# Other operation times and stated margins in the estimate that places lane steps, in a hybrid encoder layer on one core

## The chip, the cores and the metric

The kernel runs on one core of a Trainium2 chip. The core has a matrix engine (TensorE, PE in the profile), a vector engine (DVE), an activation engine (ACT), a general engine (POOL), a queue that starts most of the DMAs (SP), an on-chip memory (SBUF) and the accumulators of the matrix engine (PSUM, eight banks). Each engine works through its own instructions in the order in which the program lists them and waits on semaphores for the others. The metric is the device time of one execution in microseconds.

## The reference

One layer of a bidirectional encoder is applied to two groups of rows, 1024 sample rows and 256 prompt rows, with shared weights, in float32. All widths are 2048.

```python
hn = rms_norm(x, norm_g)
proj = hn @ w_in                       # 2048 -> 4896, split in nine parts
xbc = silu(centred_dwconv(xbc, conv_w, conv_b))
y = ssd_scan(forward) + ssd_scan(backward) + d_skip * xs     # chunks of 128 rows, 16 heads of 64
o_ssd = rms_norm(y * silu(z_ssd), per group of 512)
o_att = window_attention(q, k, v, sink) * silu(z_att)        # 8 heads, |t-s| <= 128, ALiBi
o_mem = softmax(mq @ mk.T) @ mv * silu(z_mem)                # 4 heads, 256 memory rows
return x + concat([o_ssd, o_att, o_mem]) @ w_out             # 2048 -> 2048
```

Both outputs, for the prompt rows and for the sample rows, are computed.

## The kernel before

The 1280 rows are ten tiles of 128. Tiles 0 to 4 are group 0 and 5 to 9 group 1, and each big projection is done for one group at a time. Every float32 operand of a projection is split into a high and a low part of a one-pass type, and a product is three matmuls (high x high, low x high, high x low). Weights are streamed: SP loads a tile of 128 x 512 into `wraw`, ACT copies it into the high part `wh`, DVE subtracts to get the low part `wl` (`wsplit`, lines 338 to 342).

The program has three parts. In the first, memory keys and values, the first queries, and the gate and convolution columns are projected (`seven_stage` uses seven products instead of eight, with sums of weights made on POOL). The last part is the other group's half of the output projection, in the same way. In between lies the part that the change concerns. There `block_tok` (line 368) projects the rest in blocks of 16 k steps: keys and values, memory queries, `z0` and `z1` for both groups, memory queries again, then the four output blocks of group 0. A block accumulates five row tiles in five PSUM banks (`acc`); each k step issues five times three matmuls. The three other banks, `mix`, are handed round among everything else.

Beside these main matmuls the attention and the scan have to be computed, and their work is cut into steps of Python generators in four lanes (line 252 on): ATT (`attn`, `mem_attn`, `mem_values`), SSD (`ssd_one`, `ssd_two`), PREP (norms, splits and transposes of queries and keys) and DEC (`decay`, the decay matrices of the scan). A step issues a few instructions on PE, ACT, DVE, POOL or SP, then yields what the next step wants: `wants(tiles, banks=..., after=...)` names the tiles that it reads, how many `mix` banks it takes, and earlier steps that must have been issued. A step with `banks` of one begins with matmuls or transposes on PE; one without has only ACT, DVE or POOL work.

When a step is issued decides where its instructions stand in every engine's queue. `pump` (line 301) is called after each group of three main matmuls and issues steps as long as `may` lets one through, in the order ATT, PREP, SSD, DEC. `may` asks whether the lane is owed a step by its rate, whether the `after` names have been issued, and `clk.ready`. If a step must be there and is not, `settle` and `force` issue it without that question: in `refill_o`, before the operand of an output block is loaded, and for all that is left after k step 9 of the third output block (lines 1788 to 1793).

`clk` (`Clocks`, line 43) is an estimate kept while the program is written out; nothing of it runs on the chip. It has a clock for each engine. Every instruction adds `cost` to its engine's clock, which is never behind PE's. Inside lane steps it also keeps, by tile, `full` (when what was written can be read) and `free` (when the place can be written anew); `took` passes a place's `free` on to the next tile in it, and `opens` says when the next `mix` bank is open. SP's loads are put at 2600 ns plus 1.5 ns an element of a partition. `ready` compares with PE's clock: a step goes if its tiles are full, its banks open, and ACT's and DVE's clocks at most `QUEUE`, 4000 ns, ahead. Steps without banks may go `AHEAD`, 300 ns, before their tiles are full. Steps that yield nothing to want (all of the first part's) are never held by `ready`.

The Tile framework then gives the instructions their semaphores; `wsplit` is issued with a higher priority, so that it can stand before lane work that was written out earlier.

Of the kernel before, what the change touches and what calls it, by code (L numbers as in the profile page):

```python
# [30 lines left out]

RATES = {'kv': (4, 4), 'mq0': (8, 8), 'z0': (8, 8), 'z1': (8, 8), 'mq1': (8, 8), 'o': (8, 8)}
DEBT = 6.0
AHEAD, QUEUE = 300.0, 4000.0
NEG = -1e30

UNITS = (0, 4, 1, 5, 2, 6, 7, 3, 8, 9)
# [5 lines left out]
class Clocks:  # L43
# [17 lines left out]
    def cost(self, e, ins, ops, power):  # L61
        n = max([self.size(x) for x in ops] or [1])
        if e == "PE":
            m = self.size(ops[0])
            one_pass = ops[-1].dtype == F32R or ops[1].dtype == F32R
            return m / 2.4 + 14 if one_pass else max(m / 0.6, 213) + 6
        if e == "DVE":
            return 150 + 1.05 * n
        if e == "ACT":
            return (190 + 0.8 * n if n > 16 else 190) + (190 if len(ins.outs) > 1 else 0)  # L70
        if e == "POOL":
            return 60 + 4.2 * n if n > 16 else 250 + 180 * n if power else 300
        return 50

    def ran(self, e, ins, power=False):
        outs, srcs = [[x.bass_ap for x in xs if hasattr(x, "bass_ap")] for xs in (ins.outs, ins.ins)]
        cost = self.cost(e, ins, outs + srcs, power)
        if e != "SP":
            self.now[e] = max(self.now[e], self.now["PE"])
        if not self.lane:  # L80
            self.now[e] += cost
            return
        at = self.now[e] if e != "SP" else self.now["PE"]
        for x in srcs:
            at = max(at, self.full.get(self.name(x), 0.0))
        for x in outs:
            at = max(at, self.free.get(self.name(x), 0.0))
        if e == "SP":
            end = at + 2600 + self.size(outs[0]) * 1.5
        else:  # L90
            end = self.now[e] = at + cost + 20
        for x in srcs:
            k = self.name(x)
            self.free[k] = max(self.free.get(k, 0.0), end)
        for x in outs:
            k = self.name(x)
            if e != "SP":
                self.free[k] = max(self.free.get(k, 0.0), end)
            self.full[k] = end + 90
# [10 lines left out]

    def ready(self, want):
        tiles, n = want[:2]
        at = [self.full.get(self.name(x), 0.0) - (0 if n else AHEAD) for x in tiles]
        at += [self.opens("mix", 3, i + 1) - 400 * i for i in range(n)]
        at += [self.now[e] - QUEUE for e in ("ACT", "DVE")]
        return max(at) <= self.now["PE"]

# [1755 lines left out]
```

## Time and profile before

| What | Value |
|---|---|
| Median of 3 runs | 1775.78 us (1773.38 to 1777.44) |
| Profiled execution | 1773.83 us, span 1772.1 us, granted clock 1.000 |
| PE busy | 1755.3 us, 99% of the span |
| DVE, ACT, POOL busy | 1310.9, 971.8, 683.8 us |
| Main matmuls beside the lanes, PE start to start | 0.23 us each, 512 columns |

A page shows one execution. Rows of groups give the line, the engine, the operation, the tiles written and read, the shapes, a count, busy time and mean duration, then the idle time of the engine just ahead of them and what ended it. All instructions go through one helper, so that their line is always L128, and the tile names tell them apart: `acc` and `accm` are the projections, `psc`, `ppt` and `po` scores, transposes and values of the windowed attention, `pms`, `pmt` and `pmo` the same of the memory attention, `pcb`, `pxs`, `pyf`, `pst`, `py`, `pyb` and `pr` belong to the scan, `pq`, `pk`, `pmq`, `pmk` to the preparation of queries and keys. A float32 matmul in several passes shows as two records. The end of a matmul is modelled: it is pipelined, and the next one starts well before it.

### The profile page before, as it was taken

How to read it: one execution, taken by the hardware profiler on the slowest of the kernel's cores; microseconds unless marked ns; L12 is line 12 of the kernel's file. 1: busy time of each engine (PE TensorE's matmuls, PEld its weight loads, DVE VectorE, ACT ScalarE, POOL GpSimd, SP SyncE). 2: the span in 40 equal slices, each digit the busy share in tenths (PEclk: the TensorE clock that was granted, in tenths of full speed). 3: DMA queues.
4: the chain of work that ended last, by engine and by line, in shares of the span. 5: the costliest groups of instructions: out<-in, count | busy, mean ns of one | idle time of the engine just before them, and what ended most of it. 6: DMA issues, size and time to landing. Idle time of an engine off the chain costs nothing.

```text
span 1772.1 us, 30974 instructions
## 1 busy us (share of the span) xinstructions
PE 1755.3 (99%) x10306; PEld 1572.0 (89%) x10306; DVE 1310.9 (74%) x2417; ACT 971.8 (55%) x2181; POOL 683.8 (39%) x1092
## 2 busy tenths in 40 slices
PE   9999999999999999999999999999999999999999
PEld 7889999999899999988788877887788888889999
DVE  5596788989968888797777877678776533766665
ACT  6554555445545444346787666658886532433332
POOL 0026798860478989220110000111200100068775
PEclk9999999999999999999999999999999999999999
DMA  8794454446544333376467766767785734644442
GB/s 293 238 319 175 136 149 148 128 143 194 156 119 145 119 104 106 90 216 208 143 188 249 259 213 192 226 190 230 243 249 161 222 110 147 207 142 147 145 144 77
DMA packets 210993, 313.23 MB, mean 177 GB/s; under 512 B 21584, under 2 KB 84368, under 8 KB 210832
## 3 DMA queue, kind: packets, MB, share of 16 engines
q1 hardware_dynamic: 210688, 311.19, 56.7%
q8 instruction: 81, 1.33, 0.3%
q14 instruction: 80, 0.66, 0.1%
q10 hardware_dynamic: 144, 0.06, 0.0%
HBM read 242.42 MB, written 68.75 MB: 176 GB/s over the span
## 4 chain that ended last, share of the span: by engine, by line
PE 88%; DMA 4%; DVE 3%; ACT 2%; issue 1%; POOL 1%; SPq 0%; ACTq 0%; DVEq 0%; POOLq 0%
PE acc L128 66%; PE accm L128 11%; PE py L128 2%; PE po L128 1%; PE psc L128 1%; PE pst L128 1%; PE pmo L128 1%; PE pms L128 1%; PE ppt L128 1%; DMA wraw<-in_w_in_laid_dram 1%; PE pyf L128 1%; DMA xst<-in_x_prompt_dram 1%; DVE wl L128 1%; PE pyb L128 0%; ACT lg L128 0%
## 5 line engine op out<-in xcount | busy, mean ns | idle before, releaser
L128 PE MATMUL acc<-wh,xH 128*128 128x512 f32 (+1 forms) x1248 | 490.0, 393 | 0.1
L128 DVE TENSOR_TENSOR wl<-wraw,wh 128x512 fp32r<-128x512 f32 (+1 forms) x480 | 355.5, 744 | 172.9 <-ACT wh L128 170.1
L128 PE MATMUL acc<-wl,xH 128*128 128x512 f32 (+1 forms) x1248 | 473.7, 380 | 0.7 <-DVE wl L128 0.5
L128 PE MATMUL acc<-wh,xL 128*128 128x512 f32 (+1 forms) x1248 | 472.1, 378 | 0.0
L128 ACT ACTIVATE wh<-wraw 128x512 fp32r<-128x512 f32 (+1 forms) x480 | 291.5, 613 | 211.6 <-PE acc L128 136.5
L128 POOL TENSOR_TENSOR ws<-wraw 128x128 f32<-128x128 f32 x224 | 156.9, 700 | 365.8 <-DMA wraw<-in_w_in_pairs_dram 163.1
L128 PEld LDWEIGHTS acc<-wl,xH 128*128 128x128 f32 x1248 | 234.7, 188 | 45.1 <-issue 6.5
L128 PEld LDWEIGHTS acc<-wh,xH 128*128 128x128 f32 x1248 | 234.6, 188 | 44.9 <-issue 7.0
L128 PEld LDWEIGHTS acc<-wh,xL 128*128 128x128 f32 x1248 | 234.2, 188 | 44.6 <-issue 1.0
L128 ACT ACTIVATE sh<-ws 128x384 fp32r<-128x384 f32 x224 | 115.5, 522 | 253.3 <-POOL ws L128 126.6
L128 DVE TENSOR_TENSOR sl<-ws,sh 128x384 fp32r<-128x384 f32 x224 | 158.7, 712 | 115.4 <-ACT sh L128 113.9
L128 POOL TENSOR_TENSOR ws<-wraw,ws 128x128 f32<-128x128 f32 x224 | 153.1, 683 | 17.2
L128 POOL TENSOR_TENSOR ws<-ws,wraw 128x128 f32<-128x128 f32 x224 | 154.3, 689 | 0.0
L128 POOL TENSOR_TENSOR wraw<-wraw 128x128 f32<-128x128 f32 x224 | 139.8, 624 | 17.1
L128 PE MATMUL acc<-xH,wl 128*128 128x320 f32 x320 | 100.0, 312 | 1.0 <-DVE wl L128 1.0
L128 PE MATMUL acc<-tH,sl 128*128 128x320 f32 x320 | 98.9, 309 | 0.0
L128 PE MATMUL acc<-xL,wh 128*128 128x320 f32 x320 | 98.9, 309 | 0.0
L128 PE MATMUL accm<-tH,wl 128*128 128x320 f32 x320 | 98.8, 309 | 0.0
L128 PE MATMUL acc<-tH,sh 128*128 128x320 f32 x320 | 98.7, 309 | 0.0
L128 PE MATMUL acc<-xH,wh 128*128 128x320 f32 x320 | 98.7, 309 | 0.0
L128 PE MATMUL accm<-tL,wh 128*128 128x320 f32 x320 | 98.5, 308 | 0.0
L128 PE MATMUL accm<-tH,wh 128*128 128x320 f32 x320 | 98.5, 308 | 0.0
(458 smaller groups left out, 3829.1 us busy)
## 6 DMA issues: line engine op xcount, KB each, us to landing
wraw<-in_w_in_pairs_dram SPq DMA_DIRECT2D x160, 256.0 KB, 2.7
wraw<-in_w_in_laid_dram SPq DMA_DIRECT2D x128, 256.0 KB, 3.6
wraw<-in_w_out_laid_dram SPq DMA_DIRECT2D x64, 256.0 KB, 3.1
wraw<-in_w_out_pairs_dram SPq DMA_DIRECT2D x64, 256.0 KB, 2.9
rf<-ac SPq DMA_DIRECT2D x40, 256.0 KB, 3.8
rb<-ac SPq DMA_DIRECT2D x40, 256.0 KB, 4.2
wraw<-in_w_mem_laid_dram SPq DMA_DIRECT2D x32, 256.0 KB, 4.7
ra<-in_x_turned_dram SPq DMA_DIRECT2D x16, 320.0 KB, 3.8
```

Source lines behind the costliest of these rows:

```text
L128: r = f(*a, **kw)
```

## The change

It touches constants and three functions of `Clocks`, nothing else. The costs of PE, DVE and ACT instructions are stated anew: a one-pass matmul is at least 85 ns, a float32 one counts by the share of its 128 output rows; DVE is 67 + 1.04 ns a column; ACT is 50 from PSUM or 92 from SBUF, plus 0.835 a column, 92 for each operand that is a tile beyond the first, and 92 for an accumulated sum. In a lane step the engine's clock now moves by the cost alone, and what it wrote or read is ready or free 110 ns (ACT) or 90 ns (DVE) later, where it was 20 for both clock and tile. In `ready` a step with banks waits until 700 ns after its tiles are full, a step without banks until they are full (not 300 ns before), and a bank counts as open 300 ns after its estimate.

```diff
-AHEAD, QUEUE = 300.0, 4000.0
+MARGIN, QUEUE = {"PE": 700.0, "bank": 300.0, "other": 0.0}, 4000.0
+LATE = {"ACT": 110.0, "DVE": 90.0}
...
             one_pass = ops[-1].dtype == F32R or ops[1].dtype == F32R
-            return m / 2.4 + 14 if one_pass else max(m / 0.6, 213) + 6
+            return max(m / 2.4 + 14, 85) if one_pass else max(m / 0.6, 213) * list(ops[0].ap)[0][1] / 128 + 6
         if e == "DVE":
-            return 150 + 1.05 * n
+            return 67 + 1.04 * n
         if e == "ACT":
-            return (190 + 0.8 * n if n > 16 else 190) + (190 if len(ins.outs) > 1 else 0)
+            aps = sum(hasattr(x, "bass_ap") for x in ins.ins)
+            return (50 if ops[-aps].space == "PSUM" else 92) + 0.835 * n + 92 * (aps - 1) + (92 if len(ins.outs) > 1 else 0)
...
         if e == "SP":
             end = at + 2600 + self.size(outs[0]) * 1.5
         else:
-            end = self.now[e] = at + cost + 20
+            self.now[e] = at + cost
+            end = at + cost + LATE.get(e, 20)
...
         tiles, n = want[:2]
-        at = [self.full.get(self.name(x), 0.0) - (0 if n else AHEAD) for x in tiles]
-        at += [self.opens("mix", 3, i + 1) - 400 * i for i in range(n)]
+        at = [self.full.get(self.name(x), 0.0) + MARGIN["PE" if n else "other"] for x in tiles]
+        at += [self.opens("mix", 3, i + 1) - 400 * i + MARGIN["bank"] for i in range(n)]
         at += [self.now[e] - QUEUE for e in ("ACT", "DVE")]
         return max(at) <= self.now["PE"]
```

## The prediction

> **What bounds the kernel now.** I began with the first and fourth part of the page: busy time, then the chain of work that ended last.
>
> ```profile
> span 1772.1 us, 30974 instructions
> PE 1755.3 (99%) x10306; PEld 1572.0 (89%) x10306; DVE 1310.9 (74%) x2417; ACT 971.8 (55%) x2181; POOL 683.8 (39%) x1092
> ...
> PE 88%; DMA 4%; DVE 3%; ACT 2%; issue 1%; POOL 1%; SPq 0%; ACTq 0%; DVEq 0%; POOLq 0%
> ```
>
> TensorE (PE) is busy for all but 1772.1 - 1755.3 = 16.8 us. The change issues the same instructions as before in another order, so PE's own work stays, and what it can win are PE's waits. The planner's `ready` is asked only for steps that state wants, and these lie between the last projection of keys and values and the output blocks. I took that stretch, and the 46 us behind it, from the table of stages, and then the waits of PE within the first.
>
> ```profile
> 730.00:1446.00 716.00, 706.21 (x3923) 581.08 (x3922) 526.57 (x1187) 479.59 (x1272) 80.46 (x154) 1.00 0.66 204
> 1446.00:1492.00 46.00, 46.00 (x205) 38.06 (x204) 12.40 (x19) 8.25 (x14) 0.00 (x0) 1.00 0.46 140
> ```
>
> ```profile
> engine line waited for: us in total, times, longest us
> PE py L128 <- ACT mpT L128: 2.3, 1, 2.3
> PE ppt L128 <- DVE nm L128: 1.4, 1, 1.4
> PE po L128 <- ACT pT L128: 0.9, 1, 0.9
> PE pms L128 <- DVE mql L128: 0.9, 1, 0.9
> PE pxs L128 <- DMA xc<-xbc_d: 0.8, 1, 0.8
> PE pms L128 <- DVE moT L128: 0.6, 1, 0.6
> PE acc L128 <- DVE wl L128: 0.5, 1, 0.5
> PE pacs L128 <- issue: 0.5, 1, 0.5
> PE psc L128 <- ACT st L128: 0.5, 1, 0.5
> PE pxs L128 <- DVE nm L128: 0.4, 1, 0.4
> PE pr L128 <- DVE y L128: 0.3, 1, 0.3
> PE psc L128 <- ACT pT L128: 0.2, 1, 0.2
> PE psc L128 <- ACT kL L128: 0.2, 1, 0.2
> ```
>
> In the stage (columns: PE, weight loads, DVE, ACT, POOL) PE is idle for 716.00 - 706.21 = 9.8 us; the thirteen rows hold 9.5 of them. That is little more than half a per cent of the span, and it is the whole stake. A wait costs a little more than its idle time, because the matmul ahead of it counts as busy to its end. The neighbourhood of the second row shows it.
>
> ```profile
> 865.93 0.46 PE L128 MATMUL acc<-wh,xH 128*128 128x512 f32 x1
> 866.23 0.39 PE L128 MATMUL acc<-wl,xH 128*128 128x512 f32 x1
> 866.46 0.39 PE L128 MATMUL acc<-wh,xL 128*128 128x512 f32 x1
> 868.23 0.44 PE L128 MATMUL ppt<-identr,lg 128*128 128x128 f32 x2 [1.39 <-DVE nm L128]
> 868.43 0.47 PE L128 MATMUL acc<-wh,xH 128*128 128x512 f32 x1
> 868.74 0.39 PE L128 MATMUL acc<-wl,xH 128*128 128x512 f32 x1
> ```
>
> Undisturbed, the next matmul starts 0.23 us after the one before (866.23 to 866.46) although each lasts 0.39. So every wait costs 0.16 us beside its idle time: thirteen times 0.16 is 2.1, and all waits together are worth 9.5 + 2.1 = **11.6 us**. No placement of the steps can gain much more.
>
> **The terms of the sum.** The new durations first, since both the old and the new rule decide by them. Rows of DVE and ACT working without a pause:
>
> ```profile
> 1083.03 0.68 DVE L128 TENSOR_TENSOR state<-state,cd_all 128x512 f32<-128x512 f32 x1
> 1083.62 0.69 DVE L128 TENSOR_TENSOR ya<-ya,sk 128x512 f32<-128x512 f32 x1
> 1084.22 0.42 DVE L128 CAST kT<-pk 128x256 fp32r<-128x256 f32 x1
> ...
> 1091.91 1.28 ACT L128 ACTIVATE rf<-rf,wj_all 128x128 f32<-128x128 f32 x4 [4.16 <-DMA rf<-ac]
> 1093.10 0.61 ACT L128 ACTIVATE wh<-wraw 128x512 fp32r<-128x512 f32 x1
> ```
>
> From start to start a DVE operation of 512 columns takes 0.59 to 0.60 us. The old estimate is 150 + 1.05 x 512 = 688 ns, plus 20 in a lane; the new is 67 + 1.04 x 512 = 599. Four ACT operations of 128 columns with a bias operand take 1093.10 - 1091.91 = 1.19 us, 0.30 each; old 190 + 102 + 20 = 312, new 92 + 107 + 92 = 291. So the new figures are right for spacing, and the old ones are long by about 100 ns an operation where the operation is wide. With the old ones a queue of k wide operations got about k x 0.1 us of unstated margin; now it gets a fixed one.
>
> [...]
>
> *PE steps that waited for an operand* (`po`, `pms` for `mql`, `pxs` for its load, `pr`): 2.9 us idle + 4 x 0.16 = 3.5. The old rule let them go at the estimated end plus 90 + 20; the new one adds 700 and the lag of the engine.
> - `mql`, one DVE operation of 512: 688 + 110 = 798 before, 599 + 90 + 90 + 700 = 1479 after, 0.68 later. Left of 0.9 + 0.16: 0.4.
> - `po`, two ACT copies of 256 from PSUM: 2 x 415 + 90 = 920 before, 2 x 264 + 110 + 90 + 700 = 1428 after, 0.51 later. Left of 1.06: 0.55.
> - `pxs`: the load's estimate is unchanged, so 0.70 later. Left of 0.96: 0.26. `pr`, like `mql`: nothing left.
>
> Together 3.5 - 1.2 = **2.3 us gained**.
>
> *PE steps that waited for a PSUM place* (the released engine had just emptied one of the three `mix` banks): `py`, `ppt`, `pms` for `moT`, `pxs` for `nm`, three `psc`. For one ACT copy of 512 the place opens at 190 + 410 + 20 = 620 before and 478 + 110 + 300 = 888 after, 0.27 later; with two or three wide operations queued ahead the 100 ns each have eaten that. The five small ones cost 0.6 + 0.5 + 0.4 + 0.2 + 0.2 + 5 x 0.16 = 2.7; at 0.27 less each **1.3 us are gained** if no queue stands ahead, nothing if three do (bounds 0 and 1.3). The two large ones have another cause. `py` waited for `mpT`, which stood on ACT behind the row above that was idle for 4.16 us on a load of the decay rows; the chain shows that load:
>
> ```profile
> 1083.28 8.61 DMA rf<-ac
> ```
>
> The planner gives it 2600 + 768 = 3.4 us, in both versions. What helps is only that a step of ACT or DVE is no longer sent 300 ns ahead of its operand, so that it blocks its engine 0.3 us less: **0.6 us** for the two (`ppt` I count alike, since its releaser on DVE is a long wait too; bounds 0 and 2 x 0.3).
>
> *What is not touched*: `acc` for `wl` and `pacs`, 1.0 us. *PE's estimate*: a transpose of one pass goes from 67 to 85 ns, a value product of 64 output rows from 433 to 219. It slows or speeds the planner's clock by under a microsecond a step, and moves no work.
>
> *Splitting a burst.* Behind a burst of lane steps the second main matmul starts 0.31 us after the first (868.43 to 868.74) instead of 0.23. If margins make two bursts of what was one, 0.08 us is lost; one more for each of the 20 attention and memory steps is 1.6 us, one fewer gains the same. I take 0.
>
> **Later lanes.** Every wait in a chain of steps grows. For attention with 384 keys, by the diff's formulas: scores to exponent 936 to 1112 ns, exponent to sum 1414 to 1488, sum to scaling 134 to 318, scaling to transpose 1124 to 1910, copies to values 1124 to 1642. Four quarters and two halves give 4 x 1.22 + 2 x 0.52 = 5.9 us a step, and 18 places at 0.26 another 4.7. Memory attention: low part to scores 0.68 later, scaling to transpose 0.78, copy to values 0.67, maximum to exponent 0.18, twice each, at most 4.6. This much is lost only if each wait is the last to end; the order written in the kernel interleaves four quarters, and shorter queues give some back, so I take a third: 3.5 and 1.5. Whether that costs time depends on what is behind.
>
> ```profile
> L128 PE MATMUL psc<-kT,qT x80: 274/337/447, 850.9 to 1350.1; 128*128 128x384 f32 x48, 128*128 128x256 f32 x32
> ...
> L128 PE MATMUL pms<-mkH,mqh x40: 276/283/386, 1079.1 to 1434.1; 128*128 128x256 f32 x40
> ...
> 1445.65 126.25 PE acc L128 x561
> ```
>
> First and last starts show one chain of attention steps from 850.9 to about 1445. From then on PE runs 561 main matmuls in 126.25 us, 0.225 each, with nothing between them. The kernel empties the lanes by force after ten k steps of the third output block, which leaves 6 x 15 + 240 = 330 main matmuls, 75 us before 1572, that is at about 1497. The slack is 50 us. The rear half (six attentions, ten memory steps) is late by 6 x 3.5 + 10 x 1.5 = 36 us, 110 by the upper bound. By the value I take it fits, and moving lane work into the plain stretch costs nothing, since that work is PE's own either way.
>
> **The sum.** 2.3 + 1.3 + 0.6 = 4.2 us gained. The profiled execution took 1773.83 us (span 1772.1 and 1.7 around it), so 1769.6 for its like. The median of the runs shown, 1775.78, is 1.95 above it, so I forecast **1771.6 us**, 0.24% faster. From no change a measurement of this kernel can tell about 0.2%, 3.55 us; the forecast lies just past it.
>
> **The rivals.**
> - *All waits go* (14%). The margins are long enough for every row but the load, and fewer bursts gain another 1 us: 1775.8 - 11.6 = 1764. For it: eleven of the thirteen waits are under 1 us. Against: the two largest are not of the estimate's making.
> - *Waits move, and the sum stays* (23%). The waits are thirteen single events; with the steps moved, others meet a late load or a full queue. Long queues have lost their k x 0.1 us: 1775.8 with 2 us to each side.
> - *Lanes too late, slower* (13%). If more than 50 us of delay come together, the steps left at 1497 are forced in order with no main matmul between them. A forced memory step stands on PE for its own chain: two halves of exponents, scaling and a copy, by the ACT rows below 2 x (1.12 + 1.01 + 0.59) = 5.4 us beside DVE's part, about 6. At 60 us too late (110 - 50) some three steps are left, 18 us; I price it at a step and a half with the gain kept half, +9 - 2 = 1783. The same force stands earlier, where the second-scan steps must have been done for the next operand.
>
> ```profile
> L128 ACT ACTIVATE mpr<-pms,mm,mr 128x256 f32<-128x256 f32 x40 | 22.1, 561 | 13.8 <-DVE mm L128 12.4 <-PE pyf L128 0.7 <-DVE mden L128 0.7
> ...
> L128 ACT ACTIVATE mpr<-mpr,mden 128x256 f32<-128x256 f32 x40 | 17.9, 506 | 0.0
> ...
> L128 ACT ACTIVATE mpT<-pmt 128x512 f32<-128x512 f32 x20 | 11.8, 591 | 10.0 <-PE pmt L128 10.0
> ```
>
> - *Deeper queues, slower* (7%). The limit of 4 us on ACT and DVE now holds a sixth more work, so a weight split can stand behind more of it, and the main matmuls wait for `wl`. It decides if that 0.5 us grows beyond the 4.2 gained: ten such waits of 0.9 give 9 - 4.2 = +5, 1781.
>
> **How the numbers follow.** The forecast has 43%, its own range 1768 to 1775; ten of the 43 fall within 0.2%. Faster: 33 + 14 = 47. Same: 10 + 21 of the second rival = 31. Slower: 13 + 7 + 2 = 22. The range runs from all waits gone, 1764, to the forced lanes, 1784.
>
> **What would show it.** PE's idle time in the stage falls from 9.8 to about 6; the rows for `mql`, `pT`, `y` and `xc` shrink or go; a row like `py` for a bank behind a late load remains. The last `pmo` starts later than before, near 1480, and before 1497. ACT's and DVE's operations have the same counts and durations. I am wrong if the waits for banks grow in number, if `wl` leads the list, if lane matmuls stand without main ones between them near 1497, or if the chain of the lanes ends no later than before, which would say that the margins don't set its pace.

## The result: 0.24% slower, and the profile after

The median after is 1781.69 us, against 1776.57 us for the kernel before on the same chips. The ratio is 1.0024 with a 95% interval of 1.0014 to 1.0035. The prediction said 1771.6 us and faster. Two executions in the whole record, at 2551 and 9506 us, are far off all others and count in no ratio and in no median of the table below. The profiled execution after took 1782.1 us. The first rows of its page, span and busy time:

```profile
span 1780.4 us, 30984 instructions
PE 1756.6 (99%) x10306; PEld 1570.4 (88%) x10306; DVE 1309.1 (74%) x2417; ACT 972.0 (55%) x2181; POOL 679.6 (38%) x1092
```

The engines' counts are the same, and PE is idle for 1780.4 - 1756.6 = 23.8 us, where it was 16.8: 7.0 of the 8.3 us between the two spans. (The medians differ by 5.1 us; the profiled execution of the kernel before, 1773.83 us, was one of its quicker ones.) The table of stages (span of the stretch, then PE, weight loads, DVE, ACT, POOL busy) says where. Two rows of the kernel after, and the first stretch of the kernel before, whose second the prediction shows:

```profile
0.00:728.00 728.00, 724.07 (x4465) 686.42 (x4466) 582.26 (x913) 371.30 (x698) 448.59 (x682) 1.00 0.52 165
730.00:1446.00 716.00, 700.71 (x3872) 574.64 (x3871) 523.95 (x1178) 473.90 (x1257) 79.30 (x154) 1.00 0.66 203
```

```profile
0.00:728.00 728.00, 725.65 (x4481) 689.34 (x4482) 584.95 (x916) 371.48 (x698) 451.46 (x682) 1.00 0.53 165
```

Ahead of 728 us the idle time went from 2.4 to 3.9 us. No step is held there, and the two traces list the same PE instructions in the same order up to 761 us, so this 1.6 us is one execution against another; over all profiled runs of this case, which share that order, the idle time there lies between 2.2 and 3.9 us. In the stage with the lanes it went from 9.8 to 15.3, 5.5 us more. That is the loss: from the 4700th to the 8950th matmul of PE, a stretch that holds all the lanes, the kernel after takes 6.1 us longer, which is these 5.5 us and five waits more at the prediction's 0.16. PE's waits there, of the kernel after:

```profile
engine line waited for: us in total, times, longest us
PE pxs L131 <- DMA xc<-xbc_d: 2.5, 2, 2.1
PE pk L131 <- DVE xs L131: 1.6, 1, 1.6
PE pst L131 <- DVE nm L131: 1.6, 1, 1.6
PE pmk L131 <- DMA wraw<-in_w_in_laid_dram: 1.4, 1, 1.4
PE acc L131 <- DVE wl L131: 1.4, 1, 1.4
PE psc L131 <- DVE oT L131: 1.4, 3, 1.0
PE pq L131 <- ACT pT L131: 1.3, 1, 1.3
PE pq L131 <- DVE qh L131: 1.1, 1, 1.1
PE psc L131 <- DVE xs L131: 1.0, 1, 1.0
PE psc L131 <- ACT qT L131: 0.5, 1, 0.5
PE po L131 <- ACT cb L131: 0.4, 1, 0.4
PE pxs L131 <- ACT pT L131: 0.4, 1, 0.4
PE po L131 <- DVE nm L131: 0.3, 1, 0.3
PE ppt L131 <- ACT qT L131: 0.3, 1, 0.3
PE psc L131 <- DVE ya L131: 0.2, 1, 0.2
```

Of the thirteen rows of before only `pxs` for `xc` and `acc` for `wl` are left. `mql`, `y` and the `pT` under `po` are gone, and so are `py` and `ppt` for `nm`. In their place stand others, and there are more of a microsecond.

Two rows are not what their names say. The one of `pmk` names a load of weights, which `pmk` does not read. It reads `mkr`, and DVE's last operation on that ends at 764.98 + 0.69 = 765.67, just ahead of it:

```profile
764.98 0.69 DVE L131 TENSOR_TENSOR mkr<-mkr,gm 128x512 f32<-128x512 f32 x1
...
765.87 0.63 PE L131 MATMUL pmk<-identr,mkr 128*128 128x128 f32 x4 [1.39 <-DMA wraw<-in_w_in_laid_dram]
```

And `pr` for `y` in the kernel before, which the prediction counted as an operand, is a bank: `pr` reads `yd`, while `y` is what DVE makes out of the bank of `pyb`, up to 1220.38, ahead of `pr` at 1220.43. Sorted so by what was awaited (bank: the releaser had just emptied a `mix` bank; `psc` for `qT`, 0.5 us, is counted there, though the copy that empties its bank also makes its operand):

| us of PE idle in the stage | before | after |
|---|---|---|
| a PSUM bank | 5.9 | 9.0 |
| an operand made by ACT or DVE | 1.8 | 2.5 |
| the load of the scan's columns | 0.8 | 2.5 |
| weights, other | 1.0 | 1.4 |
| sum | 9.5 | 15.4 |

What one such wait for a bank is made of shows in the timeline of the second row, DVE first, then PE:

```profile
1021.45 0.75 DVE L131 COPY_PREDICATED rb<-upper,rf 128x512 f32<-128x512 uint32 x1 [2.78 <-DMA rb<-ac]
1022.08 0.68 DVE L131 TENSOR_REDUCE qss<-sq 128x8 f32<-128x512 f32 x1
1022.66 0.68 DVE L131 SCALAR_TENSOR_TENSOR zs<-zs,acc 128x512 f32<-128x512 f32 x1
1023.26 0.42 DVE L131 CAST bth<-pcb 128x256 fp32r<-128x256 f32 x1
1023.59 0.68 DVE L131 COPY xs<-pxs 128x512 f32<-128x512 f32 x1
...
1022.31 0.39 PE L131 MATMUL acc<-wh,xL 128*128 128x512 f32 x1
1024.33 0.37 PE L131 MATMUL pk<-identr,kh 128*128 128x128 f32 x2 [1.63 <-DVE xs L131]
```

DVE stands for 2.78 us before an operation whose load of decay rows is late. Behind it wait four others in order, the last of them the copy that empties the bank; PE comes to `pk` meanwhile and waits for that bank. The estimate of DVE's durations has no part in this: they are right, and DVE was not working. `qh`, the operand under `pq` at 1043.84, is late in a like way: ACT, which makes its high part, had stood for 5.90 us until 1040.90 for a load of decay rows.

### The profile page after: what moved, and what is told of

Its sections match the earlier page's. It is cut to its first block, busy times and chain, and to the rows that moved or that the text cites. A ratio compares the mean times of both kernels' runs of the same rounds, so it can differ in the third digit from the quotient of the medians.

```text
span 1780.4 us, 30984 instructions
## 1 busy us (share of the span) xinstructions
PE 1756.6 (99%) x10306; PEld 1570.4 (88%) x10306; DVE 1309.1 (74%) x2417; ACT 972.0 (55%) x2181; POOL 679.6 (38%) x1092
## 4 chain that ended last, share of the span: by engine, by line
PE 86%; DMA 7%; DVE 2%; ACT 2%; issue 1%; POOL 1%; SPq 0%; DVEq 0%; ACTq 0%; POOLq 0%
PE acc L131 65%; PE accm L131 10%; PE py L131 2%; PE psc L131 1%; PE pst L131 1%; DMA rb<-ac 1%; PE pmo L131 1%; DMA rf<-ac 1%; PE po L131 1%; PE pms L131 1%; DMA sst<-in_x_sample_dram 1%; PE ppt L131 1%; PE pyb L131 1%; PE pyf L131 1%; DMA wraw<-in_w_in_laid_dram 1%
## 5 line engine op out<-in xcount | busy, mean ns | idle before, releaser
L131 POOL TENSOR_TENSOR ws<-wraw 128x128 f32<-128x128 f32 x224 | 152.3, 680 | 375.2 <-DMA wraw<-in_w_in_pairs_dram 167.4
L131 POOL TENSOR_TENSOR wraw<-wraw 128x128 f32<-128x128 f32 x224 | 141.6, 632 | 17.1
L131 POOL TENSOR_TENSOR es<-sinkb,nm 128x2 f32<-128x2 f32 x40 | 12.8, 321 | 234.5 <-DVE nm L131 189.0
```

What stands on the lines that cost most here:

```text
L131: r = f(*a, **kw)
```

## The experiments

Three theories stood at the start. Q: the short durations took the margin that long queues had. L: the margins make the lanes late, and that costs. R: any small change of the planner's constants deals steps, and so waits, anew (a deal is the order in which the steps come to stand), and the kernel before is one of the better deals among its neighbours. The table gives all runs. The ratio is to the kernel before on the same chip, whose medians there were 1775.7 to 1777.1 us; "waits" is the sum of the rows of PE's waits between 728 and 1520 us, "half clock" the time between 728 and 1520 us in which the granted clock was 0.50, "lanes" the start of the last value product of the memory attention. These three are of one profiled execution each. As the executions of one kernel lie up to 8 us apart, they show kinds and rough sizes, and "slower" is said of the ratios.

| Kernel | median us | ratio to before (95%) | waits us | half clock us | lanes us |
|---|---|---|---|---|---|
| before | 1776.6 | 1 | 9.5 | 0 | 1445.4 |
| after | 1781.7 | 1.0024 (1.0014 to 1.0035) | 15.4 | 0 | 1469.4 |
| estimate alone | 1789.9 | 1.0072 (1.0059 to 1.0084) | 14.0 | 6.8 | 1430.7 |
| margins alone | 1790.1 | 1.0075 (1.0063 to 1.0088) | 19.1 | 3.4 | 1496.9 |
| before, ahead 320 | 1781.6 | 1.0030 (1.0019 to 1.0041) | 14.3 | 0 | 1453.5 |
| before, ahead 310 | 1781.6 | 1.0035 (1.0021 to 1.0048) | 13.3 | 0 | 1446.2 |
| before, ahead 290 | 1787.2 | 1.0060 (1.0046 to 1.0074) | 18.9 | 6.8 | 1460.6 |
| before, queue 4100 | 1794.3 | 1.0092 (1.0079 to 1.0105) | 19.2 | 3.4 | 1443.5 |
| after, operands 720 | 1778.6 | 1.0012 (1.0003 to 1.0021) | 10.8 | 0 | 1464.9 |
| after, operands 680 | 1783.1 | 1.0040 (1.0028 to 1.0053) | 16.8 | 0 | 1458.5 |
| after, bank 320 | 1782.4 | 1.0035 (1.0023 to 1.0047) | 15.1 | 0 | 1470.8 |
| after, other -20 | 1783.6 | 1.0041 (1.0028 to 1.0055) | 13.8 | 0 | 1460.9 |
| after, queue 4100 | 1789.8 | 1.0069 (1.0055 to 1.0082) | 21.8 | 3.4 | 1473.8 |
| after, bank 900 | 1778.7 | 1.0010 (1.0002 to 1.0019) | 11.7 | 3.4 | 1464.7 |
| after, loads 5000 | 1793.2 | 1.0099 (1.0086 to 1.0112) | 17.5 | 17.1 | 1518.7 |
| after, other 380 | 1777.6 | 1.0006 (0.9997 to 1.0016) | 8.0 | 0 | 1497.9 |
| after, other 400 | 1774.2 | 0.9984 (0.9975 to 0.9993) | 7.7 | 0 | 1493.5 |
| after, other 420 | 1774.4 | 0.9990 (0.9981 to 0.9999) | 8.8 | 0 | 1494.8 |
| after, other 400, operands 720 | 1784.0 | 1.0040 (1.0028 to 1.0052) | 11.7 | 6.8 | 1494.3 |
| after, other 700 | 1787.3 | 1.0064 (1.0052 to 1.0076) | 16.9 | 3.4 | 1508.3 |

Waits and half clock together account for the stretch of the lanes. From the 4700th to the 8950th matmul of PE, every run differs from the kernel before by its idle time, 0.16 us for each wait and half of its time at half clock, to within 2 us, but for the estimate alone (3.7 us more) and the operands at 720 (2.6 us less).

**The two halves of the change.** The estimate alone, with the old margins:

```diff
-MARGIN, QUEUE = {"PE": 700.0, "bank": 300.0, "other": 0.0}, 4000.0
+MARGIN, QUEUE = {"PE": 0.0, "bank": 0.0, "other": -300.0}, 4000.0
```

> The changed kernel with the old margins (a step without a bank goes 300 ns early, 0 for operands and banks of PE steps): only the new durations and the 110/90 ns of lag are left of the change. Theory Q (the shorter durations took away the margin that long queues had, so PE meets banks and operands that are not ready): slower than the changed kernel, 1785 to 1795 us, with more PE idle time between 730 and 1500 us than its 11 us. Theory L (the margins make the lanes late, and that costs): about the kernel before, 1773 to 1778. Theory R (any new order deals the waits anew): anywhere within 1771 to 1783.

And the margins alone, in the kernel before:

```diff
-AHEAD, QUEUE = 300.0, 4000.0
+MARGIN, QUEUE = {"PE": 700.0, "bank": 300.0, "other": 0.0}, 4000.0
...
-        at = [self.full.get(self.name(x), 0.0) - (0 if n else AHEAD) for x in tiles]
-        at += [self.opens("mix", 3, i + 1) - 400 * i for i in range(n)]
+        at = [self.full.get(self.name(x), 0.0) + MARGIN["PE" if n else "other"] for x in tiles]
+        at += [self.opens("mix", 3, i + 1) - 400 * i + MARGIN["bank"] for i in range(n)]
```

> The kernel before with the new margins alone (700 ns for operands of PE steps, 300 for banks, no going ahead), its long durations kept. Theory Q: faster than before, 1768 to 1773 us, since both margins now stand together and PE's waits nearly go. Theory L: slower, 1780 to 1786, the lanes ending later than in the changed kernel (there 1468 us). Theory R: anywhere within 1771 to 1783.

Both are slower than before by three quarters of a per cent, more than the two together. The first is what Q expected, the second is the opposite of it: with the long durations and the margins, waits rose to 19.1 us. L expected the first near the kernel before. It has the earliest lanes of all, and loses 13 us. No theory of added effects gives these two and their sum. R allowed for either sign, but not for this size: it had 1771 to 1783 us for both.

**One constant moved by next to nothing.** The kernel before with `AHEAD` at 320, 290 and 310 in place of 300, and with `QUEUE` at 4100 in place of 4000:

```diff
-AHEAD, QUEUE = 300.0, 4000.0
+AHEAD, QUEUE = 320.0, 4000.0
```

> The kernel before with one constant moved by next to nothing: steps without a bank may go 320 ns ahead, not 300. Theories Q and L: 1774 to 1778 us, the same within what can be told, PE idle near 10 us in the stage. Theory R: the time moves by 3 us or more to either side, and the list of PE's waits holds other pairs.

> The kernel before, steps without a bank 290 ns ahead, not 300: a second neighbour on the other side. Theory R (a new order deals the waits anew, and the kernel before is a lucky deal): 1778 to 1785 us, as the neighbour at 320 was 1781.6. Theory S (the change itself does the harm, and 320 was an accident): 1775 to 1778.

> The kernel before with steps without a bank 310 ns ahead. Lucky deal: slower, 1779 to 1790. A smooth dependence on the constant with its best place at 300: less than half of what 320 cost, 1776 to 1779.

> The kernel before with ACT's and DVE's clocks allowed 4100 ns ahead of PE's, not 4000. If its 1776 us is a lucky deal among neighbours (320: +5, 290: +11.5), this third neighbour too is slower, 1779 to 1790. If those two were accidents of going ahead, 1774 to 1778.

All four are slower, by 0.30, 0.60, 0.35 and 0.92% (5, 11, 6 and 16 us), on both sides of 300. Ten or twenty nanoseconds of a constant are no mechanism: what they do is to let one step go a pump sooner or later, after which the rest of the lanes stands in another order. With 310, PE's instructions stand in the order of before up to 846 us, and behind that 1713 of its 10306 places hold another. Theory R expected this, and Q and L didn't; the size was beyond it in two runs, 290 (it had up to 1785 us) and the queue (up to 1790). PE's waits of the last of them, the longest rows:

```profile
PE pmt L128 <- ACT mpT L128: 2.3, 1, 2.3
PE psc L128 <- ACT qT L128: 2.3, 3, 1.2
PE pmq L128 <- DVE moT L128: 2.0, 2, 1.3
PE pr L128 <- DVE yd L128: 1.8, 1, 1.8
PE ppt L128 <- DVE nm L128: 1.7, 1, 1.7
```

None of these five stands in the list of before with more than 1.4 us, and four not at all.

The same of the changed kernel: 720 and 680 for the operands of PE steps, 320 for a bank, -20 for the steps without one, and the queue's limit at 4100.

```diff
-MARGIN, QUEUE = {"PE": 700.0, "bank": 300.0, "other": 0.0}, 4000.0
+MARGIN, QUEUE = {"PE": 720.0, "bank": 300.0, "other": 0.0}, 4000.0
```

> The changed kernel with 720 ns of margin for the operands of PE steps, not 700. Theory R: another deal, anywhere within 1774 to 1787 us, 3 us or more from the changed kernel's 1781.7 with even chance, with other pairs in the list of waits. Theory S: 1780 to 1783, the same pairs.

> The changed kernel with 680 ns for the operands of PE steps, the neighbour on the other side of 720 (which gave 1778.6). Theory R: another deal, 1774 to 1788 us, PE's idle time in its page going with it. Theory S2 (the changed estimate gives a steadier result than the old one, near 1781 with 3 us to each side): 1777 to 1784.

> The changed kernel with 320 ns of margin for a PSUM bank, not 300. The order of PE differs from the changed kernel's only from late in the lanes on, less than half as many places as in the other neighbours. Theory R: up to 4 us to either side of 1781.7. Theory S: 1780 to 1783.

> The changed kernel, steps of ACT and DVE alone let go 20 ns ahead of their tiles, not at 0: the same shift that cost the kernel before 5 us. If the two estimates are equally good on the mean of their deals: 1779 to 1793 us, like the neighbours of the kernel before (1781.6 to 1794.3). If the changed estimate is the better one and only compared with a lucky deal: 1777 to 1784, like its three neighbours so far (1778.6 to 1783.1).

> The changed kernel with the limit on ACT's and DVE's clocks at 4100 ns, not 4000: the shift that cost the kernel before 17 us. Equally good: 1779 to 1793 us. Changed estimate better: 1777 to 1784.

They lie at 1.0012, 1.0040, 1.0035, 1.0041 and 1.0069, with the changed kernel's 1.0024 among them: mean 1.0037 of six. The four neighbours of the kernel before have a mean of 1.0054, and 1.0043 with the kernel before itself. So the changed kernel is an ordinary deal of its kind, and the kernel before is better than each of its four neighbours. Whether the new estimate is the better one on the mean stays open: the means differ by 0.0017, or by 0.0006 with both kernels counted in, and the neighbours of either kernel spread by more than that (by 0.0062 for the kernel before, by 0.0057 for the changed one). The last run had been meant to tell it and fell outside what the better estimate was to give.

**More margin for a bank.**

```diff
-MARGIN, QUEUE = {"PE": 700.0, "bank": 300.0, "other": 0.0}, 4000.0
+MARGIN, QUEUE = {"PE": 700.0, "bank": 900.0, "other": 0.0}, 4000.0
```

> The changed kernel with 900 ns of margin for a PSUM bank, not 300. Theory Q: most of the new waits are for banks, so 1773 to 1777 us, and the rows of psc, pk and pq that wait for an engine that empties a bank go. Theory L: slower still, 1784 to 1792, lanes ending beyond 1480 us. Theory R: anywhere within 1773 to 1785.

1.0010 against the changed kernel's 1.0024, some 2.5 us faster, with waits of 11.7 us. Q had said 1773 to 1777 us. The rows of `pk` and `pq` went, that of `psc` did not, others for banks came (`pyb`, `pxs`), and the gain is no more than that of 20 ns of another margin. It tells Q and R apart no better than a coin.

**Loads put at 5000 ns.** Late loads stand at the head of several long waits, so the estimate of a load was raised.

```diff
-            end = at + 2600 + self.size(outs[0]) * 1.5
+            end = at + 5000 + self.size(outs[0]) * 1.5
```

> The changed kernel with a load estimated at 5000 ns plus 1.5 an element, not 2600. PE's waits for the columns of the scan (xc) were 2.5 us in the changed kernel, 4.1 with the margins alone and 2.6 in the neighbour at 320; ACT's and DVE's waits for the decay rows block both in order. Theory D (the unmodelled load is the largest steady cause of PE's waits): 1774 to 1778 us, no wait of PE for xc, and fewer waits of ACT for rf. Theory R: the waits for xc go, others come, within 1775 to 1786.

PE's waits for the scan's columns are no longer in the list, and ACT's for the decay rows went down, first the kernel after, then this one. DVE's for the decay rows did so less, from 12.3 to 9.7 us.

```profile
ACT rf L131 <- DMA rf<-ac: 15.3, 8, 5.9
```

```profile
ACT rf L131 <- DMA rf<-ac: 4.2, 3, 2.1
```

Still it is the slowest of all by its ratio, 1.0099. Here lateness seems to cost, at a place that the prediction named: the second-scan steps must have been issued by k step 11 of the last memory-query block, and those not yet done are forced there. The main matmuls of that k step end at 1236 us in this run, and the second scan (`pyb` and `pr`) follows from there to 1268, with 4.7 us of PE's waits in it. Behind it, up to 1296, stand attention steps with few main matmuls between them and another 6.5 us of waits; that they crowd there because of the force was not shown.

```profile
1200.00:1240.00 40.00, 38.32 (x194) 30.77 (x192) 25.98 (x56) 24.44 (x58) 8.68 (x14) 1.00 0.61 184
1240.00:1300.00 60.00, 50.26 (x217) 34.61 (x217) 46.99 (x97) 34.35 (x82) 10.40 (x22) 0.89 0.81 252
```

The timeline of PE in the second of these stretches:

```profile
1264.00 1.10 PE L131 MATMUL pyb<-state,cc 128*128 128x512 f32 x2 [0.83 <-DVE yd L131]
1275.36 1.62 PE L131 MATMUL pq<-identr,qh 128*128 128x128 f32 x8 [1.18 <-DVE qh L131]
1278.31 2.83 PE L131 MATMUL po<-pT,v_all 128*64 128x256 f32 x12 [1.33 <-ACT qT L131]
1295.03 0.44 PE L131 MATMUL psc<-kT,qT 128*128 128x384 f32 x1 [2.76 <-DVE oT L131]
```

In those 60 us PE is idle for 9.7, nearly as long as in the whole stage of the kernel before (9.8), and its granted clock is 0.89, by an estimate worth 60 x 0.11 = 6.6 us more.

**ACT and DVE steps held longer.** If a step that sits at the head of ACT or DVE with a late operand is the trouble, it can be sent later.

```diff
-MARGIN, QUEUE = {"PE": 700.0, "bank": 300.0, "other": 0.0}, 4000.0
+MARGIN, QUEUE = {"PE": 700.0, "bank": 300.0, "other": 400.0}, 4000.0
```

> The changed kernel with steps of ACT and DVE alone held until 400 ns after their tiles are full, not until they are. Theory H (PE's long waits for banks are steps that sit on ACT or DVE behind one whose operand is late, so holding that one back frees them): 1772 to 1778 us, ACT idle for rf and rb and PE's waits for a bank above 1 us both fewer. Theory L: the lanes end some 30 us later than in the changed kernel's 1470, near the forced end, 1783 to 1795. Theory R: 1775 to 1788 with lanes ending before 1495.

> The changed kernel, ACT and DVE steps held 380 ns after their tiles. If holding them is what helps: 1772 to 1778 us, PE's waits near 8 us like those at 400. If 400 was a lucky deal: 1776 to 1786, waits of 10 to 16 us.

> The same at 420 ns. Holding helps: 1772 to 1778 us. Lucky deal: 1776 to 1786, or more if the last steps are forced in the third output block (at 400 the last lane matmul stood at 1491.7 us).

> Held 400 ns, and 720 ns for operands of PE steps. Holding helps: 1771 to 1778 us. Lucky deal: 1776 to 1786.

> Held 700 ns. The lanes ended 24 us later at 400 than at 0, so here some 18 us later again, past k step 9 of the third output block: one or two memory steps are forced, with no main matmuls in a gap of about 4 us each (as in the run with loads at 5000 ns). Lateness past the forced end costs: 1778 to 1786 us, and fewer waits ahead of it than in the changed kernel. It does not: 1770 to 1776.

At 400 the kernel is faster than both, 0.9984 of before. PE's waits of that run, the longest:

```profile
PE pr L131 <- ACT pT L131: 1.7, 1, 1.7
PE acc L131 <- DVE wl L131: 1.3, 2, 0.7
PE pyb L131 <- DVE moT L131: 1.1, 1, 1.1
```

The neighbours at 380 and 420 have as few waits, 8.0 and 8.8 us, and 1.0006 and 0.9990, better than any neighbour at 0. So far holding helps. But with 720 for the operands beside it the time is 1.0040, and at 700 it is 1.0064, so it is no steady gain either. The reason given for it fell: ACT's wait for the decay rows was 16.7 us at 400, not less than the 15.3 of the changed kernel. In the run at 700 the lanes did end past the forced place, at 1508, and lost nothing there; its waits lie ahead. The expectation for it spoke of gaps of 4 us without main matmuls, and there are none. In five runs lane matmuls stand behind the place of the last force: 24 in those held 380, 400, 420 and 700 with operands at 700, and 60 in the run with loads at 5000. Main matmuls stand between them, and PE is busy for all of the 74 us from 1446 to 1520 in each, so the last force cost no idle time in any run.

## Why the prediction was wrong, point by point

**The step that failed** is the sum over the thirteen rows. It took each wait of before, lengthened the planner's rule for it by 0.27 to 0.70 us, and counted what was left. That holds a wait as one event which stays in its place while its length changes. It doesn't stay: the first step that goes one pump later changes every queue behind it, and the runs of the kernel before with 10 and 20 ns show that this alone moves the sum of the waits from 9.5 to between 13 and 19 us. In the changed kernel it is 15.4. The prediction had this as its second rival, with "the sum stays", 2 us to each side and 23%. That size was wrong: the four neighbours of the kernel before are 5 to 16 us slower, all to one side, as the kernel before had fewer waits than they. The profile of one kernel could not show that; but a list of single events, two of which hold 40%, could have warned of it.

- *Durations.* Right for the rows that were compared: in the kernel before the DVE rows of 512 columns at 1083 us, of 0.68 and 0.69 us, start 0.59 and 0.60 ahead of the next, where the new figure is 0.599, and in the kernel after the two at 1022.08 and 1022.66 do so 0.58 and 0.60 ahead. That made no kernel faster: the estimate alone is slower by 0.72%.
- *Operands of PE steps.* The rows that were to shrink are gone: `mql`, `pT` under `po`, and `y`, which was a bank. But two others came, `qh` under `pq` and `mkr` under the first `pmk`, and the kind went from 1.8 to 2.5 us. The load `xc` was to shrink to 0.26 and is 2.5.
- *Banks.* The rows counted as banks held 5.6 us and were to lose 1.9, of which 1.3 was the upper of its two bounds; measured 9.0. This is the term that grew most, and its sign was wrong.
- *What is not touched.* `wl` and `pacs` were to stay at 1.0 us. `wl` alone is 1.4, and `pacs` is not in the list.
- *Later lanes.* The last `pmo` record was to move by 36 us to about 1480, and moved by 24 to 1469. That the slack would hold is confirmed, and that lateness in itself costs nothing fits the runs: the earliest lanes of all (1430.7, estimate alone) belong to a kernel 13 us slower, and the fastest has them at 1493.5. The rows, before, after, estimate alone, and held 400:

```profile
L128 PE MATMUL pmo<-mpT,mv x160: 271/275/328, 1099.7 to 1445.4; 128*128 128x128 f32 x160
```

```profile
L131 PE MATMUL pmo<-mpT,mv x160: 271/275/342, 1102.4 to 1469.4; 128*128 128x128 f32 x160
```

```profile
L131 PE MATMUL pmo<-mpT,mv x160: 271/275/343, 1088.3 to 1430.7; 128*128 128x128 f32 x160
```

```profile
L131 PE MATMUL pmo<-mpT,mv x160: 271/275/377, 1126.9 to 1493.5; 128*128 128x128 f32 x160
```

- *The rivals.* "Waits move, and the sum stays" had the cause and not the sum. "Lanes too late" is not what happened: they ended at 1469, ahead of the forced place, which the main matmuls put at 1503 in this run. Its price of about 6 us for a forced memory step was seen in no run either. "Deeper queues" has a little for it, as `wl` waits 1.4 us and not 0.5, but one wait of that size is not the ten that it counted. Of the signs that were to show the forecast wrong, one came: the waits for banks grew in number, from 8 to 13.
- *The bound of 11.6 us* on any gain held: the best kernel is 2.9 us below the kernel before in its own runs (1774.2 against 1777.1).
- *The price of a wait*, idle time plus 0.16, is too low for some long ones: behind one of 2.3 us stood 3.4 us at a clock of 0.51, as the last section shows.

## What to carry to other kernels

Where an order is made by a greedy rule over estimated times, compare a change with the neighbours of the kernel before, not with the one kernel: move a constant by a hair a few times, and see how far the time goes. If that spread is larger than the effect looked for, a list of waits is a sample of single events, and the working out of each row's change is not a forecast. Where the kernel before turns out better than all its neighbours, as here, any new deal, also one from a truer estimate, is likely to start with a loss: of the nineteen other kernels here, sixteen are slower beyond their interval. Why the kernel before is so good a deal is not known.

## What the runs showed of the hardware that was not expected

**Half clock behind some waits.** In the kernel before with the queue's limit at 4100, four stretches of 3.4 us around the wait of `pmt` (PE's busy time first, the granted clock third from the end):

```profile
1086.70:1090.10 3.40, 3.40 (x26) 3.04 (x24) 2.31 (x6) 2.16 (x7) 1.43 (x2) 1.00 0.94 332
1090.10:1093.50 3.40, 1.14 (x11) 1.00 (x11) 0.82 (x2) 2.21 (x7) 0.00 (x0) 1.00 0.66 227
1093.50:1096.90 3.40, 3.40 (x11) 2.83 (x12) 1.28 (x2) 2.08 (x7) 0.00 (x0) 0.51 0.87 275
1096.90:1100.30 3.40, 3.40 (x26) 3.14 (x25) 2.15 (x6) 0.63 (x1) 0.00 (x0) 0.99 0.25 80
```

After 3.4 us in which PE was busy for 1.14, the clock is 0.51 over the next 3.4 us, and main matmuls start 0.43 us apart there instead of 0.23:

```profile
1095.07 0.63 PE L128 MATMUL acc<-wh,xL 128*128 128x512 f32 x1
1095.49 0.63 PE L128 MATMUL acc<-wh,xH 128*128 128x512 f32 x1
1095.92 0.63 PE L128 MATMUL acc<-wl,xH 128*128 128x512 f32 x1
```

By an estimate from these numbers, the half clock behind the wait of 2.3 us costs another 3.4 / 2 = 1.7 us. With the estimate alone it is 6.8 us at a clock of 0.50 behind a wait of 2.1, and nine of the eighteen experiments have such stretches in the lanes, 3.4 to 17.1 us of them by the table. Not every such wait has one behind it: in the kernel after, PE was busy for 1.26 us between 1060.4 and 1063.8, and the clock stayed at 1.00, as it did in the kernel before behind its 2.3 us for `py`. What decides it was not shown. The changed kernel's loss does not come from this, since its clock was 1.00 throughout the lanes.

**Loads that come late.** The planner puts a load of decay rows at 3.4 us. Their medians were 3.9 (`rf`) and 4.2 (`rb`) in the kernel after, and ACT stood still for one for up to 5.9 us and DVE for up to 2.8, with the emptying of banks behind. Raising the estimate to 5000 ns took most of ACT's waits away (15.3 us became 4.2) and made the lanes later (the last value product from 1469.4 to 1518.7), and that kernel is the slowest by its ratio, 1.0099, so a truer estimate of one load did not by itself make a better order.
